# Rotary embedding in a two-block model kernel: swapping halves of heads by transfers instead of by four partial products

## The chip, the cores and the metric

The kernel runs on one core of a Trainium2 chip. The metric is the device time of one execution in microseconds. One execution was also recorded by the hardware profiler; the rows below are from that one. The engines go by the names of the profile: PE is TensorE (matmul), PEld its weight load, DVE is VectorE, ACT is ScalarE, POOL is GpSimd, SP is SyncE. Each works through its own instructions in order, and they wait for one another by semaphores.

## The reference

Two blocks follow one another on 256 tokens of 1024 channels: first two layers of a convolutional mixer with a dense and a mixture-of-experts feed-forward, then one layer of attention. The change lies in the second, whose sliding-window attention rotates its queries (16 heads of 64) and keys (2 heads) by position:

```
def rope(x, pos):
    half = HEAD_DIM // 2
    inv = ROPE_THETA ** (-jnp.arange(half, dtype=jnp.float32) / half)
    ang = pos.astype(jnp.float32)[:, None] * inv[None, :]
    ...
    out = jnp.concatenate([x1 * cos - x2 * sin, x2 * cos + x1 * sin], axis=-1)

q = rope(sw_q.reshape(B, L, SWA_Q_HEADS, HEAD_DIM), pos)
k = rope(sw_k.reshape(B, L, SWA_KV_HEADS, HEAD_DIM), pos)
o_sw = sliding_window_sink_attention(q, k, sw_v..., attn_sinks[l], valid)
```

`x1` and `x2` are the two halves of a head. Beside it runs a "stick-breaking" attention with 8 heads (`sb`), and both results go through gates (z, g) and output projections.

## The kernel before

All weights come from memory once, as float32, through a ring: SyncE loads a raw tile of 1 MB (`raw`), which is two units of 128 x 1024. For each unit ScalarE rounds it to the matmul's format (`whi`, L236) and VectorE, or GpSimd for some, takes the rest (`wlo`, L238); a projection is then three matmuls for each block of 128 input channels (L351 to L353). `Stream.next` emits these two steps for the unit that is used two projections later.

In the last block (`phase_c`) activations lie with channels on the partitions, so one projection of 24 matmuls gives 128 channels of all tokens in a PSUM tile `pj`, of which there are two. A query projection holds two heads, so its 128 partitions are four halves of 32.

The order is written out by hand. The key's projection `f_k` stands ahead of the four projections of the stick-breaking queries. Then the head loop runs: for each of 8 heads, `sb1` (scores `zs`, then on ScalarE and VectorE the steps of `sb_logs` at L1822 to L1826, and `sH`), and `sb2` (matmuls `sp`, a subtraction on VectorE at L1854, an exponential on ScalarE at L1855), with a filling projection `F()` after each. The table `FILL` says which projection each `F()` takes: v, then queries (q) and gates (z) by turns, then the rest. At head 7 the first softmax of the sliding window (`sw1(0)`) begins, and then a loop over 8 pairs of heads, again with two `F()` in each.

`rope` (L1872) is in three pieces, spread over three calls of `F()`: at once, ScalarE copies the projection to `rq` (L1877; two buffers); one `F()` later, GpSimd does `turn`, which is four products of 32 partitions into `rr` (L1883; one buffer), each reading the other half of the head, then the product with the cosine (L1884) and the sum (L1885); one `F()` after that, `place` copies the result on ScalarE, twice 64 partitions (`qs`, L1630), and GpSimd takes the rests (L1631). The sine table carries the sign at the half that is read, since both inputs of a product lie on the same partitions.

Of the kernel before, what the change touches and what calls it, by code (L numbers as in the profile page):

```python
# [53 lines left out]
HD = 64  # L54
NM = 16
NK = NM + S
NEG = -float(2 ** 100)

D_T16, D_BLK, D_COS, D_SIN, D_NT2, D_NSB, D_NSW, D_TRI = 0, 128, 136, 408, 680, 696, 1096, 1496
# [1 line left out]

FILL = [(t, "kvqzqzqzqzqzqzqzqzzzzzgggggggggggggggg"[:i].count(t)) for i, t in enumerate("kvqzqzqzqzqzqzqzqzzzzzgggggggggggggggg")]


def consts_c():
    c = np.zeros((P, D_N), np.float32)
    r = np.arange(P)
    c[:, D_TRI:D_TRI + P] = r[:, None] > r[None, :]  # L70
    c[:, D_T16:D_T16 + P] = (r[:, None] // NM == r[None, :] // NM) & (r[:, None] > r[None, :])
    c[:, D_BLK:D_BLK + 8] = r[:, None] // NM == np.arange(8)[None, :]
    half = HD // 2
    inv = np.float32(10000.0) ** (-np.arange(half, dtype=np.float32) / np.float32(half))
    ang = np.arange(NK, dtype=np.float32)[None, :] * inv[r % half][:, None]
    c[:, D_COS:D_COS + NK] = np.cos(ang)

    c[:, D_SIN:D_SIN + NK] = np.sin(ang) * np.where(r % HD < half, 1.0, -1.0)[:, None]

    q = np.arange(S)[None, :] + NM  # L80
    t2 = np.arange(S - NM, S)[None, :] + NM
    c[:, D_NT2:D_NT2 + NM] = np.where(S + r[:, None] % NM < t2, 0.0, NEG)
    c[:, D_NSB:D_NSB + S] = np.where(r[:, None] < q, 0.0, NEG)
    c[:, D_NSB + S:D_NSB + 400] = np.where(P + r[:, None] < q[:, 112:], 0.0, NEG)

    k = np.arange(NK)[None, :]
    for b, (k0, k1), o in ((0, (0, 144), 0), (1, (NM, NK), 144)):
        d = (b * P + r[:, None] + NM) - k[:, k0:k1]
        c[:, D_NSW + o:D_NSW + o + k1 - k0] = np.where((d >= 0) & (d < P), 0.0, NEG)
    return c  # L90


def layout(inp):
# [19 lines left out]
    for l in range(2):  # L113
# [8 lines left out]
        for k in (4, 6, 0, 2):  # L122
# [9 lines left out]
    gu = np.concatenate([mg, mu], axis=5).reshape(NE, NCH, 2, P, 2048)  # L132
    o["w_moe"] = np.concatenate([gu, md], axis=2).reshape(NE * NCH * 3, P, 2048)
    o["consts_c"] = consts_c()
    o["meta"] = g["meta_tokens_2"]
    o["sinks"] = g["attn_sinks_2"].reshape(2, 8).T.reshape(1, 16)
# [5 lines left out]
           "z": np.concatenate([w2[:, 2816:3328], w2[:, 3328:4352][:, perm]], axis=1), "g": w2[:, 4352:6400]}  # L142
    cols += [win[t][:, i * P:(i + 1) * P] for t, i in FILL[1:]]
    w2 = np.concatenate(cols, axis=1).reshape(KD, P, 46, P).transpose(2, 1, 0, 3).reshape(46, P, 1024)
# [123 lines left out]
class K:  # L268
# [1149 lines left out]
    def phase_c(self):  # L1418
# [224 lines left out]
        make = {"v": f_v, "q": f_q, "z": f_z, "g": f_g}  # L1643
        fill = [lambda t=t, j=j: make[t](j) for t, j in FILL[1:]]
        fill = iter(fill)
# [226 lines left out]
    def rope(self, p, n, pos0, scale):  # L1872

        nc, cc = self.nc, self.cc
        qt = self.pc.tile([P, NK], F32, tag="rq", name="rq", bufs=2)
        rt = self.pc.tile([P, NK], F32, tag="rr", name="rr")
        nc.scalar.activation(qt[:, :n], p[:, :n], AF.Copy, scale=scale)  # L1877

        def turn():
            cos, sin = cc[:, D_COS + pos0:D_COS + pos0 + n], cc[:, D_SIN + pos0:D_SIN + pos0 + n]  # L1880
            for d in range(4):
                a, b = slice(32 * d, 32 * d + 32), slice(32 * (d ^ 1), 32 * (d ^ 1) + 32)
                nc.gpsimd.tensor_mul(rt[a, :n], qt[b, :n], sin[b])  # L1883
            nc.gpsimd.tensor_mul(qt[:, :n], qt[:, :n], cos)  # L1884
            nc.gpsimd.tensor_add(qt[:, :n], qt[:, :n], rt[:, :n])  # L1885
            return qt[:, :n]
        return turn
# [134 lines left out]
```

## Time and profile before

| | |
|---|---|
| median of 3 runs | 1471.13 us (1469.31 to 1471.37) |
| the profiled execution | 1470.24 us |
| its span, first to last instruction | 1468.3 us |
| TensorE busy | 1440.6 us (98%) |
| VectorE busy | 1146.8 us (78%) |
| ScalarE busy | 971.5 us (66%) |
| GpSimd busy | 266.5 us (18%) |
| mean granted clock of TensorE | 0.991 |

Matmuls are pipelined and their ends are modelled, so TensorE's busy time says only where it stood still. The shares are means over the whole program; the change touches the stretch from about 1226 to 1326 us, in the last block. A "loop" in what follows is one head of the stick-breaking part with its two projections.

### The profile page before, as it was taken

What the parts mean: (1) busy time and instruction counts of PE and PEld (TensorE: products, weight loads), DVE (VectorE), ACT (ScalarE), POOL (GpSimd) and SP (SyncE); (2) the same over time, 40 slices, a digit from 0 to 9 for tenths busy, and PEclk for the clock granted to TensorE, in tenths of its full rate; (3) what the DMA queues carried; (4) which work ended last, traced back from release to release, by engine and by line L of the source; (5) the groups of instructions that cost most, each with busy time, mean ns of one, the idle gap of its engine ahead of it and who ended that gap; (6) DMA issues with size and microseconds to landing.
All of it is one profiled execution on the core that took longest, in us unless ns stands there. A gap on an engine that the chain in (4) does not pass through costs nothing. (4 is left out here: it accounts for less than half of the span.)

```text
span 1468.3 us, 21525 instructions
## 1 busy us (share of the span) xinstructions
PE 1440.6 (98%) x8126; PEld 1234.0 (84%) x8126; DVE 1146.8 (78%) x1563; ACT 971.5 (66%) x1437; POOL 266.5 (18%) x190
## 2 busy tenths in 40 slices
PE   8999999999899999999999999999999999999997
PEld 7989999889788888888888888877888879988996
DVE  5966545579689998989999989988999966665565
ACT  5655444365587777777777777777777775756653
POOL 3750000066300000000000000000000052784511
PEclk9999999999999999999999999999999999999999
DMA  9526555444689898999999999787999824323453
GB/s 351 196 97 220 193 207 184 155 153 166 229 328 371 306 363 331 349 354 363 357 346 353 355 357 360 294 321 283 368 372 351 330 88 144 134 97 116 144 187 115
DMA packets 60049, 381.36 MB, mean 260 GB/s; under 512 B 6803, under 2 KB 7315, under 8 KB 19238
## 3 DMA queue, kind: packets, MB, share of 16 engines
q1 hardware_dynamic: 59942, 379.96, 69.7%
q8 instruction: 64, 1.05, 0.3%
q14 instruction: 43, 0.35, 0.1%
HBM read 378.89 MB, written 1.05 MB: 259 GB/s over the span
## 5 line engine op out<-in xcount | busy, mean ns | idle before, releaser
L238 DVE TENSOR_TENSOR wlo<-raw,whi 128x1024 fp32r<-128x1024 f32 x651 | 770.2, 1229 | 111.9 <-ACT whi L236 105.9
L236 ACT ACTIVATE whi<-raw 128x1024 fp32r<-128x1024 f32 x712 | 711.0, 1052 | 45.4 <-issue 16.5
L351 PE MATMUL gu<-whi,hx 128*128 128x512 f32 x704 | 285.6, 406 | 0.1
L353 PE MATMUL gu<-whi,hx 128*128 128x512 f32 x704 | 278.0, 395 | 0.0
L352 PE MATMUL gu<-wlo,hx 128*128 128x512 f32 x704 | 276.0, 392 | 0.0
L238 POOL TENSOR_TENSOR wlo<-raw,whi 128x1024 fp32r<-128x1024 f32 x61 | 147.1, 2441 | 231.7 <-ACT whi L236 229.1
L353 PEld LDWEIGHTS gu<-whi,hx 128*128 128x128 f32 x704 | 132.6, 188 | 30.7
L351 PEld LDWEIGHTS gu<-whi,hx 128*128 128x128 f32 x704 | 132.8, 189 | 26.7 <-issue 0.8
L352 PEld LDWEIGHTS gu<-wlo,hx 128*128 128x128 f32 x704 | 132.9, 189 | 25.8
L353 PE MATMUL mm<-h,wlo 128*128 128x256 f32 x512 | 144.2, 282 | 1.7 <-POOL wlo L238 1.7
L351 PE MATMUL mm<-h,whi 128*128 128x256 f32 x512 | 144.9, 283 | 0.0
L352 PE MATMUL mm<-h,whi 128*128 128x256 f32 x512 | 143.7, 281 | 0.0
L353 PE MATMUL y<-whi,aL 128*128 128x512 f32 x352 | 139.1, 395 | 1.2 <-DVE aL L346 1.2
L290 POOL TENSOR_TENSOR rs_r<-rs_v,mh 128x1 f32<-128x1 f32 (+2 forms) x21 | 18.8, 897 | 669.0 <-DVE rs_v L289 669.0
L351 PE MATMUL y<-whi,aH 128*128 128x512 f32 x352 | 139.3, 396 | 0.0
L352 PE MATMUL y<-wlo,aH 128*128 128x512 f32 x352 | 139.2, 395 | 0.0
L345 ACT ACTIVATE aH<-tr 128x256 fp32r<-128x256 f32 x90 | 34.6, 386 | 113.7 <-PE tr L1184 113.5
L351 PE MATMUL pj<-hT,whi 128*128 128x256 f32 (+1 forms) x368 | 107.3, 292 | 0.2 <-issue 0.2
L353 PE MATMUL pj<-hT,wlo 128*128 128x256 f32 (+1 forms) x368 | 104.6, 284 | 0.9 <-DVE wlo L238 0.5
L352 PE MATMUL pj<-hT,whi 128*128 128x256 f32 (+1 forms) x368 | 103.8, 282 | 0.0
L353 PEld LDWEIGHTS mm<-h,wlo 128*128 128x128 f32 x512 | 96.4, 188 | 2.7 <-POOL wlo L238 2.5
L352 PEld LDWEIGHTS mm<-h,whi 128*128 128x128 f32 x512 | 96.5, 188 | 1.4 <-issue 0.5
(383 smaller groups left out, 2316.2 us busy)
## 6 DMA issues: line engine op xcount, KB each, us to landing
raw<-w_moe SPq DMA_DIRECT2D x227, 1024.0 KB, 6.2
raw<-w_moe SPq DMA_DIRECT2D x74, 512.0 KB, 6.3
raw<-w_c SPq DMA_DIRECT2D x35, 1024.0 KB, 4.8
raw<-w_mix SPq DMA_DIRECT2D x23, 1024.0 KB, 4.9
raw<-w_gu SPq DMA_DIRECT2D x22, 1024.0 KB, 4.8
raw<-w_d SPq DMA_DIRECT2D x11, 1024.0 KB, 4.8
row<-rows SPq DMA_DIRECT2D x3, 512.0 KB, 5.6
x<-x SPq DMA_DIRECT2D x2, 512.0 KB, 5.9
```

Source lines behind the costliest of these rows:

```text
L236: nc.scalar.activation(hl[0], src, AF.Copy)
L238: (nc.gpsimd if pool is True or pool and pool[h] else nc.vector).tensor_sub(hl[1], src, hl[0].bitcast(F32))
L290: nc.gpsimd.tensor_tensor(r, v, self.mhalf[:, 0:1].to_broadcast([P, n]), op=ALU.pow)
L345: nc.scalar.activation(hi, src, AF.Copy)
L351: mm(out, a, c, start=start, stop=False)
L352: mm(out, a, d, start=False, stop=False)
L353: mm(out, b, c, start=False, stop=stop)
```

## The change

The four products of 32 partitions are replaced. ScalarE's queue now issues four transfers from `rq` to `rr`, each of 32 partitions, that swap the halves of each head, right behind the copy `rq`; GpSimd multiplies `rr` by the sine over all 128 partitions at once. The table's sign moves to the half that is written. And in `FILL` the first query comes ahead of v, so that each query is one projection sooner, and the last z later.

```diff
-FILL = [(t, "kvqzqzqzqzqzqzqzqzzzzzgggggggggggggggg"[:i].count(t)) for i, t in enumerate("kvqzqzqzqzqzqzqzqzzzzzgggggggggggggggg")]
+FILL = [(t, "kqvqzqzqzqzqzqzqzzzzzzgggggggggggggggg"[:i].count(t)) for i, t in enumerate("kqvqzqzqzqzqzqzqzzzzzzgggggggggggggggg")]
...
-    c[:, D_SIN:D_SIN + NK] = np.sin(ang) * np.where(r % HD < half, 1.0, -1.0)[:, None]
+    c[:, D_SIN:D_SIN + NK] = np.sin(ang) * np.where(r % HD < half, -1.0, 1.0)[:, None]
...
         nc.scalar.activation(qt[:, :n], p[:, :n], AF.Copy, scale=scale)
+        for d in range(4):
+            a, b = slice(32 * d, 32 * d + 32), slice(32 * (d ^ 1), 32 * (d ^ 1) + 32)
+            nc.scalar.dma_start(rt[a, :n], qt[b, :n])
 
         def turn():
             cos, sin = cc[:, D_COS + pos0:D_COS + pos0 + n], cc[:, D_SIN + pos0:D_SIN + pos0 + n]
-            for d in range(4):
-                a, b = slice(32 * d, 32 * d + 32), slice(32 * (d ^ 1), 32 * (d ^ 1) + 32)
-                nc.gpsimd.tensor_mul(rt[a, :n], qt[b, :n], sin[b])
+            nc.gpsimd.tensor_mul(rt[:, :n], rt[:, :n], sin)
             nc.gpsimd.tensor_mul(qt[:, :n], qt[:, :n], cos)
             nc.gpsimd.tensor_add(qt[:, :n], qt[:, :n], rt[:, :n])
```

The lines of the changed file are lower by one from L78 up to `rope`. ScalarE's instructions in one loop of the head loop, before (`lb L1855` is the exponential of `sb2`, L1822 to L1824 and `sH` belong to `sb1`, `pj` is a projection):

```order
L236 ACTIVATE whi<-raw 128x1024
L1877 ACTIVATE rq<-pj 128x256
L1630 ACTIVATE qs<-rq 64x256 x2
L1855 ACTIVATE lb<-lb 128x400
L236 ACTIVATE whi<-raw 128x1024
L1637 ACTIVATE z<-pj 128x256
L1822 ACTIVATE lb<-zs 128x400
L1823 ACTIVATE lb<-lb 128x400
L1824 ACTIVATE lb<-lb,ones 128x400
L1839 ACTIVATE sH<-s 128x400
```

The same stretch of ScalarE's order after the change:

```order
L235 ACTIVATE whi<-raw 128x1024
L1876 ACTIVATE rq<-pj 128x256
L1879 DMA rr<-rq 32x256 x4
L1629 ACTIVATE qs<-rq 64x256 x2
L1821 ACTIVATE lb<-zs 128x400
L1822 ACTIVATE lb<-lb 128x400
L1823 ACTIVATE lb<-lb,ones 128x400
L1838 ACTIVATE sH<-s 128x400
L235 ACTIVATE whi<-raw 128x1024
L1636 ACTIVATE z<-pj 128x256
L1854 ACTIVATE lb<-lb 128x400
```

The query's copy and the copies `qs` have changed places with the gate's copy z: they stood ahead of the exponential of `sb2` and now stand ahead of `sb1`'s steps, and four issues stand between them.

GpSimd's instructions for the first query, from the last one for the key, before:

```order
L1600 CAST k_10671<-k_10671 64x272
L1883 TENSOR_TENSOR rr<-rq,cc 32x256 x4
L1884 TENSOR_TENSOR rq<-rq,cc 128x256
L1885 TENSOR_TENSOR rq<-rq,rr 128x256
L1631 TENSOR_TENSOR qs<-rq,qs 64x256 x2
```

and after:

```order
L1599 CAST k_10671<-k_10671 64x272
L1883 TENSOR_TENSOR rr<-rr,cc 128x256
L1884 TENSOR_TENSOR rq<-rq,cc 128x256
L1885 TENSOR_TENSOR rq<-rq,rr 128x256
L1630 TENSOR_TENSOR qs<-rq,qs 64x256 x2
```

One product stands where four stood, and it now reads `rr`, so it waits for the transfers.

## Rows read from the trace of the kernel before

**Rows 1.** The page, the chain that ended last, by line.

```profile
POOL rr L1883 2%; PE pj L351 2%; PE pj L353 1%; PE pj L352 1%; POOL qs L1631 1%; POOL wlo L238 1%; POOL rq L1885 1%; PE pw L353 1%; PE pw L352 1%; PE pw L351 1%; PE acc L352 0%; PE acc L353 0%; PE acc L351 0%; ACT whi L236 0%; POOL rq L1884 0%
```

**Rows 2.** Busy time by stretch: stretch, length, engines (instructions), clock, DMA share, GB/s.

```profile
1260.00:1280.00 20.00, 20.00 (x163) 19.45 (x162) 11.20 (x14) 13.95 (x27) 17.83 (x19) 1.00 0.32 119
```

**Rows 3.** Waits of ScalarE, 1225 to 1345 us: total, times, longest.

```profile
ACT qs L1630 <- POOL rq L1885: 12.9, 6, 4.5
...
ACT q L1608 <- PE pj L353: 5.1, 4, 1.5
...
ACT w L1814 <- DVE w L1813: 1.2, 1, 1.2
```

**Rows 4.** Timeline of ScalarE, one loop: start, length, line, [idle before <- releaser].

```profile
1251.88 0.37 ACT L1877 ACTIVATE rq<-pj 128x256 f32<-128x256 f32 x1
1253.74 0.54 ACT L1855 ACTIVATE lb<-lb 128x400 f32<-128x400 f32 x1 [1.50 <-DVE lb L1854]
...
1257.77 0.54 ACT L1839 ACTIVATE sH<-s 128x400 fp32r<-128x400 f32 x1 [0.64 <-DVE s L1825]
...
1259.17 0.36 ACT L1877 ACTIVATE rq<-pj 128x256 f32<-128x256 f32 x1
1259.43 0.84 ACT L1630 ACTIVATE qs<-rq 64x256 fp32r<-64x256 f32 x2
```

**Rows 5.** Timeline of VectorE, between two steps of that loop.

```profile
1252.00 1.23 DVE L238 TENSOR_TENSOR wlo<-raw,whi 128x1024 fp32r<-128x1024 f32 x1 [0.37 <-ACT whi L236]
1253.15 0.56 DVE L1854 TENSOR_TENSOR lb<-lb,sp 128x400 f32<-128x400 f32 x1
```

**Rows 6.** Timeline of TensorE: first and sixth `zs`, and a projection's first `wlo`.

```profile
1252.99 0.35 PE L1833 MATMUL zs<-nR,iR 128*128 128x400 f32 x1
...
1254.09 0.28 PE L353 MATMUL pj<-hT,wlo 128*128 128x256 f32 x1
...
1293.02 0.34 PE L1833 MATMUL zs<-nR,iR 128*128 128x400 f32 x1
```

**Rows 7.** Waits of TensorE, 1300 to 1330 us; then one stretch, columns as in rows 2.

```profile
PE ov L1982 <- DVE pt L1966: 2.1, 1, 2.1
PE pT L1964 <- DVE pr L1953: 1.2, 2, 0.7
PE pT L1964 <- DVE pr L1954: 0.7, 2, 0.4
PE pj L353 <- DVE wlo L238: 0.5, 1, 0.5
...
1320.00:1325.00 5.00, 4.44 (x25) 3.94 (x24) 2.08 (x9) 2.88 (x11) 0.00 (x0) 0.72 0.55 210
```

**Rows 8.** Groups by line, GpSimd, 1240 to 1345 us: busy, mean ns | idle before.

```profile
L1883 POOL TENSOR_TENSOR rr<-rq,cc 32x256 f32<-32x256 f32 x32 | 31.4, 982 | 12.6 <-ACT rq L1877 10.6
L1631 POOL TENSOR_TENSOR qs<-rq,qs 64x256 fp32r<-64x256 f32 x16 | 13.1, 817 | 11.3 <-ACT qs L1630 10.7
L1885 POOL TENSOR_TENSOR rq<-rq,rr 128x256 f32<-128x256 f32 x8 | 9.6, 1195 | 0.6
...
L1884 POOL TENSOR_TENSOR rq<-rq,cc 128x256 f32<-128x256 f32 x8 | 6.7, 842 | 0.6
```

**Rows 9.** Timeline of SyncE's queue at the start of the program.

```profile
0.91 0.39 SPq L410 DMA_DIRECT2D x<-x  x1
1.35 0.32 SPq L413 DMA_DIRECT2D g<-rows  x1
...
7.05 0.56 SPq L455 DMA_DIRECT2D bd<-consts  x1
```

**Rows 10.** DMA issues by line: count, KB each, median us from issue to landing.

```profile
raw<-w_c SPq DMA_DIRECT2D x35, 1024.0 KB, 4.8
...
out<-xn SPq DMA_DIRECT2D x4, 256.0 KB, 2.1
...
sg<-sgu_b SPq DMA_DIRECT2D x2, 256.0 KB, 7.6
```

## Prediction, made before the changed kernel ran

> **What bounds the kernel now.** I read the chain of waits first: in the last block GpSimd's rotation leads it, with `rr L1883` at 2% of the span, `qs L1631` and `rq L1885` at 1% each [rows 1]. That looks like 4% to be won. The busy times of stretches say how little of it is: between 1260 and 1280 us TensorE is busy for all 20 us, GpSimd for 17.83, ScalarE for 13.95 [rows 2]. The chain ends there on GpSimd because the last softmax waited for it, but TensorE, fed with weights, hardly noticed. So the prize is not GpSimd's time but the few places where TensorE stood still for its sake. Between 1300 and 1330 us they are five short gaps, 0.5 + 1.2 + 0.7 = 2.4 us (for `wlo` and for the `pr` of the first softmax), and one of 2.1 for `pt`; and the granted clock is 0.72 from 1320 to 1325, a mix of the levels 2.4 and 1.2 GHz [rows 7].
>
> The link between GpSimd and TensorE is ScalarE. It rounds every weight (`whi`), evacuates every projection, runs the exponentials and copies the rotated queries (`qs`), all in one order. Its wait list shows 12.9 us in six waits for GpSimd's `rq`, the longest 4.5 [rows 3]. So the question is what ScalarE's order looks like after the change.
>
> **ScalarE's loop, before.** One loop holds two projections, one of them a query's, and one head of the stick-breaking part. Between two copies `rq`, at 1251.88 and 1259.17, ScalarE needs 7.29 us [rows 4]; this is the one loop with no `qs` pair in it and no wait for GpSimd. In it stand two waits that are no accident: 1.50 us before `lb L1855` and 0.64 before `sH`. The first is VectorE's: `wlo` starts when `whi` is done and takes 1.23 us, and the subtraction `lb L1854`, queued behind it, 0.56 [rows 5]. Whatever follows a `whi` on ScalarE and precedes `lb L1855` is therefore free up to some 1.5 us. Before the change a query's `rq` and the `qs` pair (0.84 us) stand in just that place, and so does the wait for GpSimd.
>
> TensorE's loop, from one `zs` at 1252.99 to the sixth at 1293.02, is 40.03 / 5 = 8.01 us [rows 6]. ScalarE at 7.29 plus little is inside it.
>
> **GpSimd's part.** Each query loses four products of 32 partitions at 0.98 us and gains one of 128, which I price like its neighbour `rq L1884`, 0.84: 3.1 us less. With `rq L1884` (0.84), `rq L1885` (1.20) and the two `qs` at 0.82 [rows 8], GpSimd needs 4.5 us in a loop instead of 7.6, and it no longer sets anything. If the new product cost as much as two old ones, 5.6 would still be under TensorE's 8. The sine table's sign moves to the other half at no cost.
>
> **The transfers on ScalarE's queue.** The trace of before has no transfer issued by ScalarE and none between two on-chip tiles, so issue and landing are bounded by SyncE's. Its first two start 0.44 us apart; the second takes 0.32, with the gap of 0.05 between them 0.37 [rows 9]: about 0.40, for a tile of 128 x 1024 and for one row of it alike. Bounds for one issue: zero (the queue may run beside the arithmetic, since nothing shows a ScalarE issue at all) and 0.56, for a 128 x 128 load behind others [rows 9]. I take 0.40, because the first two agree over a hundredfold range of size. Four of them are 1.60 us. They wait for the copy `rq` they read to be finished: a copy lasts 0.36 and its follower starts 0.26 after it, so 0.10 more. Everything behind them on ScalarE waits: `qs`, three steps of `sb_logs`, `sH`, the next `whi`, and through `whi` VectorE and TensorE.
>
> The Trainium skill, page "DMA: Bandwidth & Descriptors", section "Issuing engines are not separate DMA queues", says that a queue's time to start a transfer is usually small beside the transfer. The trace agrees in the ratio (0.40 against 4.8 us) but 0.40 is more than the 0.26 that a copy holds ScalarE. With the issues at zero, as the rule may be read, the sum below would be -2.0 instead of +8.1.
>
> Landing: issued to landed is 2.1 us for 256 KB of output, 4.8 for a weight of 1 MB, 7.6 for the slowest kind [rows 10]. I take 2.1, the row nearest in size to 32 KB. The copy starts at 0, the last issue ends at 1.96, data are there at about 4, GpSimd's three operations of 2.9 us end near 7. The next query's transfers, which write the single buffer `rr` again, are issued a loop later, so that wait costs nothing up to a landing of some 5 us.
>
> **The order.** With "kqvqz" a query's projection is the first of a loop where it was the second. This moves `rq`, and now four issues and the `qs` pair, from ahead of `lb L1855` to ahead of `sb_logs`. There nothing waits that would hide them. Ahead of `lb L1855` stands the copy of z, and the 1.50 us of wait is bare again, as in the loop of [rows 4]. So the new loop is that loop with rq and z exchanged, plus what comes in: 7.29 + 1.60 + 0.10 + 0.84 = 9.83 us against TensorE's 8.01. TensorE must wait 1.82 us a loop for `whi` and `wlo`. The queries q1 to q6 do so in full: 6 x 1.82 = 10.9. The issues for q0 fall in the first projection, ahead of the exponential of `w`, where 1.2 us of wait lie [rows 3]: 1.70 - 1.2 = 0.5 more. The lead that TensorE has at the start goes off: `wlo` was ready at 1253.23 for its matmul at 1254.09 [rows 5, 6], 0.9. The key's four issues stand in the projections ahead of all this, where ScalarE waits for the matmuls of q, 5.1 us in four waits [rows 3]; these hide 1.70 us, and I cost it at zero (without them it would be the 1.7 once).
>
> What comes back: the five gaps, 2.4 us together, follow ScalarE's long waits for GpSimd, the last of 4.5 us. I take them as gone. The gap of 2.1 stays, as it follows the second softmax (`sc`, exponential, transposes), whose order on ScalarE and VectorE is as before. The slow clock would give back up to 0.28 x 5 = 1.4 us; but gaps of nearly 2 us a loop can lower it again, and I count it at nothing.
>
> **Sum.** 10.9 + 0.5 - 0.9 - 2.4 = +8.1 us. The profiled execution took 1470.24 us, its span 1468.3, the rest is outside; the median of the runs shown is 1471.13, within 1 us of it. 1471.1 + 8.1 = **1479 us**.
>
> **Rivals.** (1) The forecast, ScalarE-bound loops, slower. With issues between 0.25 and 0.56 us the loop is 9.23 to 10.47 us and the sum 6 x 1.22 - 3.3 = +4.0 up to 6 x 2.46 + 1.1 - 3.3 = +12.6 (3.3 for lead and gaps, 1.1 for q0's issues): 1475 to 1484. 66%.
>
> (2) Issues are nearly free on ScalarE: its queue hands them on beside the arithmetic. With 0.10 us each the loop is 8.63, 6 x 0.62 - 3.3 = +0.4. What returns at the end pays for the longer loops, and up to 0.2 us an issue the time is within 2.9 us of the old one, 1469 to 1474. For it: no row shows ScalarE being held. Against: SyncE is held each time [rows 9]. The sign turns at 0.08 us an issue. 14%. (The rule of the Trainium skill named above speaks for this one.)
>
> (3) Faster. The issue costs nothing, ScalarE falls back by 0.22 us a loop, 1.3 in all, of which the lead takes 0.9, and it comes to the first softmax without its wait of 4.5 us. Then 1.3 - 3.3 = -2.0, the clock's 1.4 comes back too, and the 2.1 for `pt` in part: 3.4 to 5.5 us, so 1466 to 1468. It needs issues well under 0.08 us. For it speaks that the chain runs through GpSimd [rows 1], against it that ScalarE's bare wait comes back whatever an issue costs. 12%.
>
> (4) The transfers land late, behind weights on the same DMA engines. At 7.6 us the copy-to-sum time is 1.96 + 7.6 + 2.9 = 12.5 us, more than a loop, and ScalarE's next issue waits for `rr`: 6 x 4.5 less 3 is +24, some 1495; it begins at a landing of some 5 us, with weights at 4.8 the median. Against it: the DMA engines are a third busy there [rows 2], and 32 KB is little. 8%.
>
> **The numbers.** A measurement of this kernel tells about 0.2%, 2.9 us, from no change. Slower by more: 66 + 8 = 74%. Within: 14%. Faster: 12%. The range leaves out the faster rival and the late landing, 20%: from 1470 (issues nearly free) to 1487 (issues of 0.56, some clock lost on top).
>
> **What would show it.** Right: on ScalarE's queue four issues behind each `rq`, 0.35 to 0.45 us apart, and 1.5 us of wait before `lb L1855` (now L1854) again; `rq` to `rq` 9.5 to 10 us; TensorE with about six gaps of 1 to 3 us, put down to `wlo`, between 1260 and 1315; no wait of ScalarE for GpSimd; GpSimd under half busy. Wrong in the step of the issues: they are 0.1 us apart and the loop is under 8.7. Wrong in the step of the order: the wait for `lb` has shrunk although `qs` no longer stands before it. Wrong in landing: ScalarE's first issue waits for GpSimd. The whole would be wrong if TensorE's loop stayed at 8.0 us.

## The result: slower, and by more than predicted

| | before | after |
|---|---|---|
| median | 1470.88 us (4 runs) | 1489.32 us (4 runs, 1486.53 to 1492.52) |
| ratio | | 1.0127, 95% interval 1.0115 to 1.0139 |
| profiled span | 1468.3 us | 1485.7 us |
| mean granted clock | 0.991 | 0.987 |

The change costs 18.4 us. Slower was the forecast, at 1479 us; the time lies 2 us above the range's upper end of 1487. In after `qs` is L1629 and the exponential of `sb2` L1854.

The chain that ended last no longer runs through GpSimd, and yet the kernel is slower. Its shares by engine, first before, then after:

```profile
PE 12%; POOL 4%; ACT 2%; DVE 1%; issue 1%; POOLq 0%; ACTq 0%
```

```profile
PE 9%; DVE 1%; ACT 1%; issue 0%; ACTq 0%; POOL 0%; POOLq 0%
```

The timeline of ScalarE in after, one loop from a query's copy `rq` to the next (start, length, engine and line, what it does, idle time before and its releaser; ACTq is its DMA queue):

```profile
1268.97 0.36 ACT L1876 ACTIVATE rq<-pj 128x256 f32<-128x256 f32 x1
1269.41 2.44 ACTq L1879 DMA_DIRECT2D rr<-rq  x4
1271.89 0.85 ACT L1629 ACTIVATE qs<-rq 64x256 fp32r<-64x256 f32 x2 [2.56 <-issue]
1272.77 0.50 ACT L1821 ACTIVATE lb<-zs 128x400 f32<-128x400 f32 x1
1273.31 0.54 ACT L1822 ACTIVATE lb<-lb 128x400 f32<-128x400 f32 x1
1273.88 0.63 ACT L1823 ACTIVATE lb<-lb,ones 128x400 f32<-128x400 f32 x1
1275.15 0.54 ACT L1838 ACTIVATE sH<-s 128x400 fp32r<-128x400 f32 x1 [0.64 <-DVE s L1824]
1275.59 1.04 ACT L235 ACTIVATE whi<-raw 128x1024 fp32r<-128x1024 f32 x1
1276.54 0.37 ACT L1636 ACTIVATE z<-pj 128x256 f32<-128x256 f32 x1
1276.80 0.38 ACT L1869 ACTIVATE o<-av 128x256 f32<-128x256 f32 x1
1278.41 0.54 ACT L1854 ACTIVATE lb<-lb 128x400 f32<-128x400 f32 x1 [1.23 <-DVE lb L1853]
1278.86 1.04 ACT L235 ACTIVATE whi<-raw 128x1024 fp32r<-128x1024 f32 x1
1279.81 0.37 ACT L1876 ACTIVATE rq<-pj 128x256 f32<-128x256 f32 x1
```

The loop is 10.84 us, and in it ScalarE never waits for TensorE or GpSimd. Its one long stop is `2.56 <-issue`: it is sending off four transfers, 0.61 us each. The wait before `lb L1854` stands bare again, 1.23 us, with the query's copies gone from ahead of it. The loop of [rows 4] took 7.29 us.

The waits of ScalarE in after, 1225 to 1365 us (total, times, longest), beside [rows 3]:

```profile
ACT qs L1629 <- issue: 18.7, 7, 3.2
ACT lb L1854 <- DVE lb L1853: 12.5, 8, 2.2
...
ACT whi L235 <- issue: 2.7, 1, 2.7
...
ACT w L1813 <- issue: 2.5, 1, 2.5
...
ACT k L1593 <- POOL rq L1885: 1.0, 1, 1.0
```

The 12.9 us that `qs` waited for GpSimd are gone; one wait of 1.0 us for it is left, at the key's copy `k`. In their place stand 18.7 us of issuing, and 12.5 for VectorE.

TensorE pays for it. Its waits in after, 1225 to 1420 us, then two of its gaps, then the stretch of the head loop (columns as in [rows 2]), first before, then after:

```profile
PE pj L350 <- ACT z L1636: 8.4, 4, 2.9
...
PE ov L1982 <- DVE pt L1966: 3.0, 1, 3.0
...
PE pj L352 <- DVE wlo L237: 2.9, 6, 0.8
```

```profile
1266.06 0.58 PE L350 MATMUL pj<-hT,whi 128*128 128x256 f32 x1 [2.85 <-ACT z L1636]
1267.12 0.58 PE L352 MATMUL pj<-hT,wlo 128*128 128x256 f32 x1 [0.27 <-DVE wlo L237]
```

```profile
1260.00:1315.00 55.00, 54.45 (x437) 52.41 (x435) 35.16 (x44) 36.73 (x75) 48.78 (x51) 1.00 0.33 120
```

```profile
1260.00:1330.00 70.00, 58.96 (x401) 55.26 (x401) 30.23 (x39) 39.35 (x74) 28.54 (x32) 0.88 0.35 115
```

Most gaps are put down to the copy `z`, which frees the PSUM tile of a projection, and only the short ones behind them to `wlo`. Both come from the same late ScalarE. Before, 0.55 us of 55 were idle and the granted clock was 1.00. In after 11 us of 70 are idle, and the granted clock is 0.88, a mix of its levels 2.4 and 1.2 GHz.

### The profile page after: what moved, and what is told of

Same layout as the page of the kernel before. It is cut to its first block, busy times and chain, and to the rows that moved or that the text cites. A ratio compares the mean times of both kernels' runs of the same rounds, so it can differ in the third digit from the quotient of the medians.

```text
span 1485.7 us, 21581 instructions
## 1 busy us (share of the span) xinstructions
PE 1452.4 (98%) x8126; PEld 1243.7 (84%) x8126; DVE 1138.2 (77%) x1563; ACT 971.6 (65%) x1437; POOL 238.4 (16%) x163
## 5 line engine op out<-in xcount | busy, mean ns | idle before, releaser
L237 DVE TENSOR_TENSOR wlo<-raw,whi 128x1024 fp32r<-128x1024 f32 x651 | 767.2, 1225 | 115.9 <-ACT whi L235 109.0
L350 PE MATMUL pj<-hT,whi 128*128 128x256 f32 (+1 forms) x368 | 110.4, 300 | 8.6 <-ACT z L1636 8.4
L352 PE MATMUL pj<-hT,wlo 128*128 128x256 f32 (+1 forms) x368 | 107.9, 293 | 3.0 <-DVE wlo L237 2.9
L351 PE MATMUL pj<-hT,whi 128*128 128x256 f32 (+1 forms) x368 | 106.8, 290 | 0.0
```

What stands on the lines that cost most here:

```text
L237: (nc.gpsimd if pool is True or pool and pool[h] else nc.vector).tensor_sub(hl[1], src, hl[0].bitcast(F32))
L350: mm(out, a, c, start=start, stop=False)
L351: mm(out, a, d, start=False, stop=False)
L352: mm(out, b, c, start=False, stop=stop)
```

## The experiments

**The order alone.** The kernel before with the new table; GpSimd keeps its four products.

```diff
-FILL ... "kvqzqzqzqzqzqzqzqzzzzzgggggggggggggggg"
+FILL ... "kqvqzqzqzqzqzqzqzzzzzzgggggggggggggggg"
```

> The kernel before with the new table alone (kqvqz), the rotation left as four products on GpSimd. Theory of the issues (ScalarE is held 0.61 us by each of its four issues where nothing hides it): without issues ScalarE's loop is 7.29 + 0.84 for the pair qs = 8.1 us, TensorE's 8.0, so within 3 us of before: 1468 to 1474. Rival, the order by itself is the loss: 1479 or more.

Measured: 1468.83 us, ratio 0.9988 (0.9979 to 0.9998). ScalarE's loops are mostly 8.35 to 8.44 us (8.63 in the mean of seven), and none waits for GpSimd. So the order by itself is not the loss; with the long rotation it gains 2 us. Two projections lie between a query's copy and its `qs` in either order; what differs is that ScalarE now comes for the result every 8.4 us, where in the first two loops of before it came after 7.3, and GpSimd was reckoned at 7.6. That this is where the 2 us come from was not tried.

**The transfers in the old order.** The changed kernel with the old table (the same edit, reversed).

> The changed kernel with the old table (kvqz), transfers still issued by ScalarE. Theory of the issues with the place: ahead of the exponential of sb2 some 1.5 us of the issues lie in a wait for VectorE, so the loop falls from 11.0 to about 9.5 us; but copy, issues, landing and sums take about 10 us, and the single rr makes the next issue wait for that, so 9.5 to 10 us a loop and 1480 to 1484. Rival, the order is the loss: back to 1471. Rival, ScalarE's place is indifferent: 1489.

Measured: 1476.09 us, ratio 1.0039 (1.0025 to 1.0053), less than the 1480 to 1484 that the theory expected. The timeline of ScalarE, its middle part:

```profile
1269.80 0.36 ACT L1876 ACTIVATE rq<-pj 128x256 f32<-128x256 f32 x1
1270.23 2.56 ACTq L1879 DMA_DIRECT2D rr<-rq  x4
1272.84 0.86 ACT L1629 ACTIVATE qs<-rq 64x256 fp32r<-64x256 f32 x2 [2.68 <-issue]
1273.72 0.39 ACT L1869 ACTIVATE o<-av 128x256 f32<-128x256 f32 x1
1274.12 0.54 ACT L1854 ACTIVATE lb<-lb 128x400 f32<-128x400 f32 x1
```

The issues are as long as in after, but they stand ahead of `lb L1854`, and its wait has vanished: it is spent on issuing. The loop is 9.07 us in the mean of seven, against 11.05. So the change of order is worth 2 us a loop and 13.2 us in all with the issues in it; 2.1 of these the order costs without any issue (last run below), so about 11 belong to the issues' place.

**Two issues, one, none.** In the new order. These three leave out the swap of the halves within a head, so the count can be changed.

```diff
-        for d in range(4):
-            a, b = slice(32 * d, 32 * d + 32), slice(32 * (d ^ 1), 32 * (d ^ 1) + 32)
+        for d in range(2):
+            a, b = slice(64 * d, 64 * d + 64), slice(64 * (d ^ 1), 64 * (d ^ 1) + 64)
```

> The changed kernel with two transfers of 64 partitions in place of four of 32; the same bytes, but halves of 64 are swapped, so the rotation is computed with the wrong partner. Theory of the issues: 2 x 0.61 = 1.22 us less on ScalarE, loop 9.8 us, 6 x 1.22 and once 1.2 less: 1480 to 1482. Rival, an issue's length grows with its partitions, or the landing and not the issue sets the loop: 1487 to 1490.

```diff
-        for d in range(4): ...
-            nc.scalar.dma_start(rt[a, :n], qt[b, :n])
+        nc.scalar.dma_start(rt[:, :n], qt[:, :n])
```

> Leaves out: the swap (one transfer copies all 128 partitions straight, so the queries are turned wrongly). One issue on ScalarE in place of four, with the same 128 KB. Theory (each issue holds ScalarE about 0.6 us, whatever it moves): loop 8.9 to 9.1 us; on the line through two issues (1478) and four (1489.3), 5.7 us an issue, this gives 1472.3: 1471 to 1474. Rival (the first issue carries a fixed cost, the wait for the copy or for the landing, and the others little): 1475 or more. Rival (length goes with bytes): the one issue lasts 2 us or more and the time is that of two or four issues.

```diff
-        for d in range(4): ...
-            nc.scalar.dma_start(rt[a, :n], qt[b, :n])
...
-            nc.gpsimd.tensor_mul(rt[:, :n], rt[:, :n], sin)
+            nc.gpsimd.tensor_mul(rt[:, :n], qt[:, :n], sin)
```

> Leaves out: the swap of the halves (the sine product reads the copied queries themselves, so they are turned wrongly). Order of the projections and GpSimd's three products are those of the changed kernel; no transfer and no issue is left. Theory (ScalarE's loop is the bound, and what lengthens it is the four issues): ScalarE's loop from rq to rq is 8.3 to 8.6 us, as with the order alone, and the time is 1467 to 1470 us; this is the prediction's sum with issues at zero, -2.0. Rival (part of the loss is in the order with the shorter rotation, or in the clock): 1473 or more.

| issues behind a query's copy | one lasts (median) | ScalarE's loop, mean of 7 | time |
|---|---|---|---|
| 0 | | 8.48 us | 1466.82 us |
| 1 of 128 partitions | 0.47 us | 8.90 | 1470.66 |
| 2 of 64 | 0.57 | 9.87 | 1477.98 |
| 4 of 32 (after) | 0.61 | 11.05 | 1489.32 |

The one issue in a line (timeline of ScalarE):

```profile
1273.80 0.36 ACT L1876 ACTIVATE rq<-pj 128x256 f32<-128x256 f32 x1
1274.25 0.47 ACTq L1877 DMA_DIRECT2D rr<-rq  x1
1274.77 0.85 ACT L1629 ACTIVATE qs<-rq 64x256 fp32r<-64x256 f32 x2 [0.60 <-ACT rq L1876]
```

The bytes are the same in the last three rows of the table, so the price goes by the number of issues and not by the bytes: 3.8 us for the first, 7.3 for the second, 5.7 each for the next two. The partitions of an issue change along with the number, and the first issue of a row is the shorter one (0.51 us in the next run, the one behind it 0.61), so the table does not say what a single issue of 32 partitions lasts. All three came out below what was expected: two issues by 2 us (1480 to 1482), though their loop is the 9.8 us expected, one by 0.3 (1471 to 1474), none by 0.2 (1467 to 1470). Without issues the kernel is 3.6 us faster than before (0.9978, 0.9969 to 0.9988).

**Idle issues.** The order-alone kernel, with its four products, and beside them four small transfers from a constant that nobody reads.

```diff
+        ru = self.pc.tile([P, 8], F32, tag="ru", name="ru")
+        for d in range(4):
+            a, b = slice(32 * d, 32 * d + 32), slice(32 * (d ^ 1), 32 * (d ^ 1) + 32)
+            nc.scalar.dma_start(ru[a, :], cc[b, D_COS:D_COS + 8])
```

> The kernel before with the new order of projections (1468.8), with GpSimd's four products kept, and behind each copy rq four transfers issued by ScalarE of 32 partitions x 8 numbers of a constant into a tile that nobody reads. So it has the issues alone: nothing waits for a landing and GpSimd has the old work. Theory (the issues themselves hold ScalarE): 0.5 to 0.65 us each, loop 10.5 to 11 us, 1484 to 1491. Rival (what costs is the landing, or the way over the single tile rr): 1468 to 1473.

Measured: 1477.55 us, 8.7 above the order alone. This lies between the expectations, 6.5 us under the theory's and 4.5 over its rival's: the issues cost time with no landing to wait for, but about half of what the theory gave them. The timeline shows where the other half went:

```profile
1273.68 0.54 ACT L1855 ACTIVATE lb<-lb 128x400 f32<-128x400 f32 x1 [1.75 <-DVE lb L1854]
1273.91 0.51 ACTq L1881 DMA_DIRECT2D ru<-cc  x1
1274.13 1.04 ACT L236 ACTIVATE whi<-raw 128x1024 fp32r<-128x1024 f32 x1
1274.45 0.61 ACTq L1881 DMA_DIRECT2D ru<-cc  x1
1275.08 0.36 ACT L1877 ACTIVATE rq<-pj 128x256 f32<-128x256 f32 x1
1275.10 1.25 ACTq L1881 DMA_DIRECT2D ru<-cc  x2
1276.39 0.86 ACT L1630 ACTIVATE qs<-rq 64x256 fp32r<-64x256 f32 x2 [0.95 <-issue]
```

In the program the four issues stand behind `rq`. Depending on nothing just computed, they begin while the arithmetic ahead of them still runs: the first lies under `lb` and `whi`, the second under `whi`, and the third begins under `rq`. The four take 2.37 us here too, but the loop grows by 1.1 (means of seven, 9.75 against 8.63). In after the issues read the copy `rq`, begin only behind its end, and no arithmetic stands beside them in the timeline. So an issue's length on ScalarE is about 0.6 us, and its price to the loop between 0.28 and all of it, by what stands around it.

**SyncE issues the transfers**, in the new order and in the old.

```diff
-            nc.scalar.dma_start(rt[a, :n], qt[b, :n])
+            nc.sync.dma_start(rt[a, :n], qt[b, :n])
```

> The changed kernel with the same four transfers issued by SyncE. Theory of the issues: ScalarE's loop is 7.29 + 0.84 = 8.1 us and TensorE's 8.0, so 1470 to 1474, with hardly a gap of TensorE. Rival, the landing sets the loop: the transfers land 4 us after the last issue, the sums end 9 to 10 us after the copy, ScalarE's pair qs waits 1 to 2 us a loop for them: 1477 to 1483. Rival, SyncE is held up and weights come late: waits of whi for raw.

> The changed kernel with the four transfers issued by SyncE and the old order of the projections. Theory (with the issues off ScalarE only the landing is left, and in the old order it lies beside VectorE's low half, 1.5 us, and one more step): ScalarE's waits for GpSimd's rq under 4 us in all, 1468 to 1472. Rival (the landing costs its 4.5 us in any order): 1474 to 1477.

Measured: in the new order 1475.48 us, ratio 1.0029 (1.0019 to 1.0038), between the expectations; in the old order **1463.00 us, 0.9954 (0.9938 to 0.9971)**, faster than both kernels and than the 1468 to 1472 expected. What sets the two apart is SyncE's queue. First the new order, where ScalarE's copies `rq` begin at 1257.40 and 1267.31:

```profile
1258.79 0.33 SPq L218 DMA_DIRECT2D raw<-w_c  x1
1259.39 2.41 SPq L1879 DMA_DIRECT2D rr<-rq  x4
1268.69 0.33 SPq L218 DMA_DIRECT2D raw<-w_c  x1
1269.26 2.65 SPq L1879 DMA_DIRECT2D rr<-rq  x4
```

Then the old, with copies at 1259.40 and 1266.68:

```profile
1259.82 2.41 SPq L1879 DMA_DIRECT2D rr<-rq  x4
1264.04 0.33 SPq L218 DMA_DIRECT2D raw<-w_c  x1
1267.11 2.44 SPq L1879 DMA_DIRECT2D rr<-rq  x4
```

In the new order a weight load stands just ahead of the transfers. It waits for its buffer (52.0 us in eight waits for `wlo`, 1240 to 1330 us), the transfers wait behind it, 1.6 us past the end of the copy, and then they land beside its megabyte. Their median from issue to landing is 4.1 us, in the old order, where the last load was issued 3 us earlier, 1.9. With ScalarE issuing, the medians are the same, 4.1 us in the new order (after) and 1.9 in the old, though the loads are SyncE's. That the DMA engines are shared, whoever issues, is what the Trainium skill says, page "DMA: Bandwidth & Descriptors", section "Issuing engines are not separate DMA queues"; these four numbers agree. ScalarE then waits for the late sums, in the new order (first fence, waits from 1225 to 1365 us), and not in the old (second):

```profile
ACT qs L1629 <- POOL rq L1885: 8.2, 4, 2.6
```

```profile
ACT qs L1629 <- POOL rq L1885: 0.2, 1, 0.2
```

In the old order TensorE is kept fed to the end. Busy time by stretch, first before, then SyncE's transfers in the old order (columns as in [rows 2]):

```profile
1290.00:1320.00 30.00, 27.47 (x216) 25.56 (x215) 19.93 (x30) 16.76 (x37) 25.94 (x29) 0.99 0.29 106
1320.00:1350.00 30.00, 27.36 (x218) 25.59 (x217) 18.15 (x58) 16.83 (x50) 12.93 (x7) 0.95 0.31 107
```

```profile
1290.00:1320.00 30.00, 29.44 (x243) 28.39 (x242) 18.68 (x38) 20.04 (x51) 14.41 (x17) 1.00 0.39 130
1320.00:1350.00 30.00, 29.48 (x250) 27.91 (x249) 19.83 (x60) 17.39 (x51) 15.06 (x7) 1.00 0.31 107
```

There are 4.1 us less of idle TensorE, and a clock of 1.00 in place of 0.99 and 0.95, by estimate worth 0.01 x 30 + 0.05 x 30 = 0.3 + 1.5 us: together 5.9 of the 7.5 us. Once more, with more runs:

> The four transfers issued by SyncE in the old order once more, for a closer interval: 1462 to 1464.5 us, a ratio of 0.995 to 0.996 with an interval that stays under 0.998.

Measured: 1463.60 us, 0.9953 (0.9939 to 0.9966).

**No transfers, old order**, to see whether anything of the transfers is left in that time (edits as in the run without transfers, with the old table).

> Leaves out: the swap of the halves, as in the run without transfers, but with the old order of the projections. Theory (TensorE bounds the loops of the old order once ScalarE has no issue and no wait for GpSimd; SyncE's transfers in the old order are fully hidden): the time is that of SyncE's transfers in the old order, 1463.0, within 2 us, and ScalarE's loop 7.5 to 7.7 us. Rival (the landing still costs something there): 1459 to 1460. Rival (the old order is in itself the slower one): 1465 or more.

Measured: 1464.70 us, 0.9959 (0.9944 to 0.9974), ScalarE's loop 7.58 us in the mean, both as expected. The transfers from SyncE are hidden whole in the old order. And without issues the new order (1466.82) is 2.1 us slower than the old: what the order itself costs with the short rotation.

Seen together, the same four transfers cost nothing (SyncE, old order), 9 us (SyncE, new), 11 us (ScalarE, old) or 22.5 us (ScalarE, new), each against the kernel without transfers in its order.

## Why the prediction was right in kind and wrong in size

**GpSimd: right.** ScalarE's waits for it at `qs`, its share of the chain and the five gaps of [rows 7] went as said; no `PE pT` wait is left in after. It is busy 28.54 of 70 us, under half.

**The order: right.** The bare wait came back (1.23 to 1.63 us a loop from q1 on) and `qs` lost its cover. The loop without issues was worked out as 7.29 + 0.84 = 8.13 (8.23 with the 0.10 of waiting for the copy); the kernel without transfers has 8.43 from q1 to q7. The sum with issues at zero was -2.0 us; that kernel measures -3.6. This is near, but not by the same terms: its loop is longer than reckoned, and it has a clock of 1.00 from 1320 to 1350 us, where before has 0.95, which the sum left out. The key's issues were put at nothing and cost little: from the key's copy to q0's it is 18.45 us in after and 18.12 without transfers.

**The issue: the step that failed.** It was taken at 0.40 us from SyncE's first two issues of the program, with an upper bound of 0.56 from a later one [rows 9]. Measured over the 36 issues of after (minimum, median, maximum in ns):

```profile
L1879 ACTq DMA_DIRECT2D rr<-rq x36: 514/612/1267, 1229.4 to 1327.0; - x36
```

The median is 0.61 us, outside the bounds. It is not ScalarE that is slow: SyncE needs 0.58 for the same transfers (median of 36), and 0.33 for a weight load in the rows above. The trace of before had no transfer from one on-chip tile to another. But it had loads on SyncE's queue that take longer than the bound, between the rows of [rows 9]:

```profile
4.03 1.66 SPq L451 DMA_DIRECT2D cp<-cp  x1
...
6.30 0.70 SPq L453 DMA_DIRECT2D con<-consts  x1
```

So two rows that agreed were chosen out of a spread from 0.32 to 1.66 us, their agreement over sizes was no support for the value, and 0.56 was no upper bound. What makes one issue longer than another, no run here shows.

In the sum this is 4 x 0.21 = 0.84 us a loop, 5.0 over six loops, and 0.8 for q0 (2.5 us of wait at `w` against the 1.7 taken). By itself it would have made 1485 us, still inside the range; smaller parts carry the time out of it. The loops measured from q1 to q7 are 66.68 / 6 = 11.11 us against the 9.83 predicted, so 0.44 a loop, 2.6 in all, is not the issues' length. It is made of 0.30 that the loop without issues is longer (8.43 against 8.13), 0.08 more between copy and first issue, and 0.11 from one set of issues that took 3.10 us, together 0.49 and so 0.05 too much. The gap for `pt`, taken as unchanged, grew from 2.1 to 3.0. With these, 6 x 3.10 + 1.3 - 0.9 - 2.4 + 0.9 = +17.5, against 17.4 between the two profiled spans; the lead of 0.9 in it no run measures by itself, so the closeness is in part luck. The medians differ by one more.

**The clock: left out, and no loss by it is seen.** The granted clock fell to 0.88 between 1260 and 1330 us, where TensorE has its gaps. In the loop shown ScalarE has no wait for TensorE, so the slower matmuls may have filled time in which TensorE would have stood. That is argued from the rows and was not tried by itself.

**TensorE's releaser: half right.** The gaps came, the four long ones 1.35 to 2.85 us, but were put down to the PSUM tile freed by `z`, not to `wlo`. The predicted sign was too narrow: the copy stands behind `whi` in ScalarE's order, so when ScalarE is late it is the copy that ends the wait.

**The rivals.** Nearly free issues fell with the table of 0, 1, 2 and 4. Late landing did not decide in after: ScalarE's only wait for GpSimd there is the 1.0 us at the key, although the median landing of 4.1 us is twice the 2.1 taken. It does cost time where SyncE issues in the new order. The faster rival needed issues that cost nothing, and when they do, the gain it named is there: 1466.8 us without transfers, in its 1466 to 1468, and 1463 from SyncE in the old order.

The rule of the Trainium skill weighed in the prediction (page "DMA: Bandwidth & Descriptors", section "Issuing engines are not separate DMA queues"), that starting a transfer takes little beside the transfer, holds as a ratio (0.61 against 4.1 us) and misleads here: four starts in a row hold ScalarE for 2.44 us of a 10.84 us loop, at a place where its time is the bound.

## What to carry to other kernels

Here the price went by the issues and not by the bytes. Count the issues, and put them on a queue whose engine has time; on a computing engine, put them where it waits anyway or where they do not depend on the instruction just before. When an issue moves to a shared queue, look at what stands ahead of it there: here a load that waited for its buffer delayed the transfers behind it, and they landed later. An order that is right for a slow producer can be wrong for a fast one: with four products on GpSimd the new order gained 2 us, with one it lost 2. So try the two edits of such a change apart.

## What was not expected of the hardware

- An issue of an on-chip transfer holds the queue for 0.47 us (128 partitions, alone) to 0.61 us (32 partitions, four in a row) on ScalarE and 0.58 on SyncE (32 partitions, four in a row), where a weight load of 1 MB is issued in 0.33.
- The same 32 KB land in 1.9 us (median) where the last load of 1 MB was issued 3 us before, and in 4.1 us right behind one.
- ScalarE runs an issue beside the arithmetic of the instructions ahead of it, if the issue does not wait for their result: the first of four began 1.2 us before the copy that stands ahead of it in the program. Such issues, 2.37 us long, lengthened the loop by 1.1; those that read the copy, 2.44 us long, by 2.6.
